# Half-block copies and z's stores move to ScalarE, and norm sums get y's bank 0.15 slots later: a prediction and its test

## The chip, the core and the metric

The kernel runs on one core of a Trainium2 chip. The core's engines each run one stream of instructions in order and meet at semaphores: TensorE (PE in the profile, with its weight loads as PEld), VectorE (DVE), ScalarE (ACT), GpSimd (POOL), and SyncE (SP), which here only issues DMAs. The metric is device time in microseconds for one execution, as the median of several.

## The reference

One layer of an encoder block on 2048 positions of width 1024. One wide projection of the normalized input gives the queries, keys and values of two attention mixers and their gates. Both mixers normalize each head of q and k, add a table of relative positions to the scores, and take a softmax over a window.

```python
h = rms_norm(x, norm_gain[layer])
proj = h @ w_in[layer]
qa, ka, va, qb, kb, vb, ga, gb, mg = jnp.split(proj, split_idx, axis=-1)
qa = head_rms_norm(qa.reshape(bsz, S, A_Q_HEADS, HEAD_DIM), q_norm_a[layer]) * scale
...
ya, _ = banded_attention(qa, ka, va, A_WINDOW, 1, rel_bias[:, :A_Q_HEADS], sink_a[layer])
ya = ya.reshape(bsz, S, A_WIDTH) * jax.nn.silu(ga)
...
for g, (window, dilation) in enumerate(B_GROUPS):      # (128, 1), (512, 4), (2048, 16)
    o, l = dilated_group(qb[:, :, g], kb[:, :, g], vb[:, :, g], window, dilation, ...)
alpha = jax.nn.softmax(jnp.stack(lses, axis=0), axis=0)
yb = jnp.sum(alpha[..., None].astype(x.dtype) * jnp.stack(outs, axis=0), axis=0)
yb = yb.reshape(bsz, S, B_WIDTH) * jax.nn.silu(gb)
...
merged = gates[:, :, 0] * br_a + gates[:, :, 1] * br_b
x = x + merged @ w_out[layer]
```

## The kernel before

**Numbers as pairs.** Operands of matmuls are split into a 16-bit high part and a 16-bit rest, so each product is three matmuls: high by high, high by rest, rest by high (XH, XL for the input; wh, wl for weights).

**Stages.** First the input is normalized, transposed and split. Then comes the long stage that the change touches: 14 units, each a group of heads, with 8 slots per unit. At the end the branches are projected, merged and sent through the output projection.

**Units.** A unit is "A" (mixer A, two units) or "B" with a group g of the three dilations. For each of four pairs of heads the order is g = 1, g = 2, g = 0. A unit's tokens are taken in blocks of 128: g = 1 has four sequences of four blocks, g = 2 sixteen sequences of one block, g = 0 one sequence of 16 blocks. In g = 1 and g = 0 a query's window begins half a block early, so key blocks are placed half a block off from the query blocks.

**A slot.** In each slot TensorE projects a pair of blocks into two banks of PSUM, pj: 2 x 24 matmuls on line 654. For each bank, ACT evacuates q and k (L672) and v's high part (L687), and DVE v's rest (L693), which empties the bank. For the pair, in this order: ACT squares (L700), DVE sums and guesses a reciprocal root (L705, L706, L262), POOL refines it in three rounds (newton, L271 to L274), DVE scales (L717), POOL multiplies by the gain (L724), ACT rounds to the high part (L730), DVE takes the rest (L734), POOL swaps the parts of k (L739), and SP transposes both blocks by DMA (L747) into a ring of eight blocks, kq, in two rows of four. Where one row ends and the next begins, the window of a query needs a half block again in the other row, or at the end of its own: `edge` copies it, 0.45 slots after the transpose. There are 36 such copies: per pair of heads 4 in g = 1 (L759) and 5 in g = 0 (L763, three of L757, L766). In slots of some units TensorE also does projections of gates as "fills" (L309).

**Attention of a block.** About three slots after its pair began: scores into PSUM (PE, L832), bias and maximum (DVE, L847), exponential (ACT, L855), high part and rest (ACT L860, DVE L864), transpose by DMA (SP, L870), values (PE, L881), and evacuation by ACT: L900 for mixer A, L905 for g = 0, and for g = 1 and 2 L909 into a tile z, which `z_store` sends to memory (L916, 0.1 slots later, 128 stores). In g = 0 the stored parts are read back (L890) and the three groups are merged: DVE makes factors (L1019 to L1032), POOL multiplies (three products per two blocks, L1037), DVE adds (L1043, L1044).

**The bank pt.** One bank of PSUM serves two uses in turn. `YPart.turn` transposes a finished part of y into it (PE, L943), and `YPart.gate` multiplies it by the gate (DVE, L947). Norm sums of weights, of gates and of y (`norm_sum`, L195, two tiny matmuls) use it too. The flag `held` keeps one from being placed between the other's write and read; a step that finds it set tries again 0.04 slots later.

**Order.** The order of each engine's instructions is written out by hand: steps are put on a heap with a due time in slots (`at`), and `until` takes them from it between two matmuls. The constants at the top are such times. The program then waits only through semaphores.

Of the kernel before, what the change touches and what calls it, by code (L numbers as in the profile page):

```python
# [24 lines left out]
AF = mybir.ActivationFunctionType  # L25
# [52 lines left out]
G_PREP = (5.907, 6.882, 7.102, 7.671, 7.712, 7.812, 7.942)  # L78
N_PREP = (6.3, 7.15, 7.753)
B_GAP = (0.25, 0.138, 0.231)  # L80
Y_MAX = (0.026, 0.815, 0.839)
X_SQ = (5.098, 1.401, 9.779, 2.051)
X_CH = (9.3, 2.65, 1.024, 0.955, 1.155, 1.305)
# [29 lines left out]
def block_kernel(tc, x, w_units, w_gate, w_mrg, w_brn, w_out, w_bra, gain, qkg, sink, bias_a, bias_b, b_merge, out):  # L113
    nc = tc.nc
    V = nc.vector
    A = nc.scalar
    G = nc.gpsimd
# [69 lines left out]
    held = [False, True]  # L187
# [128 lines left out]
    def g_load(c, raw=None, parts=(0, 1)):  # L316
        if raw is None:
            raw = sp0.tile([128, NCH, 128], F32, name="graw", bufs=2)[:]
        for i in parts:
            nc.sync.dma_start(out=raw[:, 4 * i:4 * i + 4, :], in_=w_gate[c][:, 4 * i:4 * i + 4, :])  # L320
        gw[c] = [raw]
# [44 lines left out]
    def gate_steps(ps, c, q, ih, m):  # L366
        th = []

        def tanh():
            th.append(gp.tile([128, 512], F32, name="yo", bufs=3))  # L370
            if m is None:
                A.activation(th[0][:], ps[:], AF.Tanh, scale=ih[:])
            else:
                i = 8 * (m % 2) + m // 2
                A.activation(th[0][:], ps[:], AF.Tanh, bias=bmh[:, i:i + 1], scale=ih[:])

        def gate():
            if m is None:
                V.scalar_tensor_tensor(th[0][:], th[0][:], 1.0, ps[:], OP.add, OP.mult)

        def store():
            d = gtd[c] if m is None else mgd[m]
            nc.sync.dma_start(out=d[:, 512 * q:512 * q + 512], in_=th[0][:])
            done.add(("gt", c, q))

        return tanh, gate, store
# [4 lines left out]
    def at(t, f, *args):  # L391
        seq[0] += 1
        heapq.heappush(heap, (t, seq[0], f, args))

    now = [0.0]
# [6 lines left out]
    def chain(steps):  # L402

        steps = sorted(steps, key=lambda e: e[0])
        done = [0]

        def go(k):
            if done[0] < k or steps[k][1](*steps[k][2:]) is False:
                at(now[0] + .04, go, k)
            else:  # L410
                done[0] = k + 1

        for k, e in enumerate(steps):
            at(e[0], go, k)
# [220 lines left out]
    ring = wk.tile([128, 6, 2 * RING], F16, name="kq", bufs=1)  # L635
    blocks = [0]

    class Pair:
# [113 lines left out]
        def edge(self, r, c, o):  # L752

            un = self.un
            if c:
                e = RING * (o < RING) + 512
                G.tensor_copy(ring[:, :un.nq, e:e + 64], ring[:, :un.nq, o:o + 64])  # L757
            elif un.n == 4:
                G.tensor_copy(ring[:, :, o + 512:o + 576], ring[:, :, o:o + 64])  # L759
                un.kq[r, 4] = ring, o + 512  # L760
            else:
                first = wk.tile([128, 6, 64], F16, name="kq0", bufs=1)
                G.tensor_copy(first[:], ring[:, :, o:o + 64])  # L763
                un.kq[r, un.n] = first, 0
            if c and c + 4 == un.n:
                G.tensor_copy(ring[:, :un.nq, o + 512:o + 576], un.kq[r, un.n][0][:, :un.nq, :])  # L766


    class Item:
# [142 lines left out]
        def z_store(self):  # L912
            un = self.un
            dst = zd[un.idx][un.g - 1].rearrange("(j d) f -> d j f", d=un.d)[
                self.r, 128 * self.i:128 * self.i + 128, :]
            nc.sync.dma_start(out=dst, in_=self.z[:].rearrange("p h f -> p (h f)"))  # L916
            done.add(("z", un.idx, un.g, self.r, self.i))


    class YPart:  # L920
# [10 lines left out]
        def plan(self, t):  # L931
            steps = [(t + d, f) for d, f in zip(Y_PART, (self.load, self.turn, self.gate, self.top, self.store))]
            if self.q == 3:
                steps += [(t + Y_PART[3] + d, f) for d, f in zip(Y_MAX, (self.max1, self.max2, self.max3))]
            chain(steps)

        def turn(self):
# [4 lines left out]
            for b in range(4):  # L942
                T.transpose(self.ps[:, 128 * b:128 * b + 128], self.y[:, b, :], idf[:])  # L943

        def gate(self):
            held[0] = False
            V.scalar_tensor_tensor(self.o[:], self.ps[:], gw[self.chunk][2][:], self.o[:],  # L947
                                   OP.mult, OP.mult)

# [139 lines left out]
    for u in range(NU + 1):  # L1089
        t = 8 * u  # L1090
        steps = [(t + W_STEP[0] + B_GAP[0] * i, w_load, u + 1, (i,)) for i in range(4)]
        for i in range(4):
# [6 lines left out]
    for c, u, slots in FILLS:  # L1099
# [6 lines left out]
        for i in range(2):  # L1106
            at(t + G_PREP[0] + B_GAP[1] * i, lambda u=u, c=c, i=i: g_load(c, pre[u][0], (i,)))
        chain([(t + G_PREP[1] + .1 * i, g_gain, c, i) for i in range(2)]
              + [(t + d, f, c) for d, f in zip(G_PREP[2:], (g_square, g_sum, g_pow, g_hi, g_lo))])
    for k in range(8):  # L1110
# [4 lines left out]
        for j in range(4):  # L1115
            at(t + N_PREP[0] + B_GAP[2] * j, piece_load, u, k, j)
        for half in range(2):
# [5 lines left out]
    un, nxt = None, 0.0  # L1123
    t = 0
    while t < NPAIR or heap or any(k >= t for k in fill):
        u, j = divmod(t, 8)
        steps = [(f, args) for f, *args in fill.pop(t, [])]
        if u < NU:
            if j == 0:
                un = Unit(u)  # L1130
# [5 lines left out]
            e = [t + 3.9 / (7.8 + 5.2 * len(steps)), t + 7.8 / (7.8 + 5.2 * len(steps))]  # L1136
# [272 lines left out]
    def gate_group(n):  # L1409
# [43 lines left out]
        def two(ps):  # L1453
            d = tile_()
            plus(d, ps, a, 1.0)
            gate(d, d, 0, 0, T_S[8])

        steps = ((A11, B11, lambda ps: copy(a, ps, 1.0)), (A12, B21, two), (S1, T1, lambda ps: copy(b, ps, 16.0)),
                 (S2, T2, lambda ps: (plus(c, ps, a, 16.0), add(a, b, c))),
                 (S3, T3, lambda ps: (plus(c, ps, c, 16.0), add(b, b, c), gate(b, b, 1, 2, T_S[7]))),  # L1460
                 (S4, B22, lambda ps: (plus(a, ps, a, 4.0), gate(a, a, 1, 0, T_S[8]))),
                 (A22, N4, lambda ps: (plus(c, ps, c, 4.0), gate(c, c, 0, 2, T_S[8]))))
# [106 lines left out]
    def branch_pair(i, dc, q):  # L1569
        set_, col = (i // 3, i % 3) if i < 6 else (2, i - 6)  # L1570
        assert ("br", set_) in done and all(("y", c, q) in done for c in range(8))
        for k in range(2):
            ps = ps_p.tile([128, 512], F32, name="fps")

            def product(ps=ps, k=k):
                g = gates[dc, q, k]
                V.scalar_tensor_tensor(g[:], g[:], 1.0, ps[:], OP.add, OP.mult)

            e = job(2.6, tproj_list(ps, *bw[set_][1:3], 128 * col, 0, 4, YS[q][0], YS[q][1], 4 * k))
            at(e + T_GATE[1], product)  # L1580

        def merge():
            m = gates[dc, q, 0]
            G.tensor_tensor(m[:], m[:], gates[dc, q, 1][:], OP.add)
            kept[dc, q] = m[:]

        at(e + T_GATE[2], merge)
        return e
# [12 lines left out]
    for k, (i, q) in enumerate(steps):  # L1601
        e = branch_pair(i, BCS[i], q)
        if k + 3 < len(steps):
            at(e + T_GATE[3], gate_load, BCS[steps[k + 3][0]], steps[k + 3][1])
        p = (i // 2, q % 2)
# [168 lines left out]
```

## Time and profile before

| | us |
| --- | --- |
| median of three runs | 1957.76 (1952.71 to 1959.26) |
| the profiled execution, its own time | 1958.9 |
| its span, first to last instruction | 1956.9 |
| PE busy | 1926.9 (98%) |
| DVE busy | 1377.4 (70%) |
| ACT busy | 1063.0 (54%) |
| POOL busy | 971.2 (50%) |

How to read it: times are microseconds from the start of the span. "L757" is line 757 of the kernel. A row of the timeline gives start, length, engine, line, operation, the tiles written and read, their shapes, and how many were merged; in square brackets stands how long the engine was idle before and what ended that. A row of waits gives who waited for whom, the total, the number of times and the longest. A row of a group has the busy time and the mean in ns behind the first bar. A row of one tile or line has minimum, median and maximum in ns. In rows of SP the length is that of the issue, not that of the transfer. The granted clock is TensorE's, as a share of its full speed.

### The profile page before, as it was taken

What the parts mean: (1) busy time and instruction counts of PE and PEld (TensorE: products, weight loads), DVE (VectorE), ACT (ScalarE), POOL (GpSimd) and SP (SyncE); (2) the same over time, 40 slices, a digit from 0 to 9 for tenths busy, and PEclk for the clock granted to TensorE, in tenths of its full rate; (3) what the DMA queues carried; (4) which work ended last, traced back from release to release, by engine and by line L of the source; (5) the groups of instructions that cost most, each with busy time, mean ns of one, the idle gap of its engine ahead of it and who ended that gap; (6) DMA issues with size and microseconds to landing.
All of it is one profiled execution on the core that took longest, in us unless ns stands there. A gap on an engine that the chain in (4) does not pass through costs nothing.

```text
span 1956.9 us, 40345 instructions
## 1 busy us (share of the span) xinstructions
PE 1926.9 (98%) x13702; PEld 1213.0 (62%) x13702; DVE 1377.4 (70%) x3604; ACT 1063.0 (54%) x2415; POOL 971.2 (50%) x2476
## 2 busy tenths in 40 slices
PE   8999999999999999999999899999999999999999
PEld 5556666677766688666787567876444444444444
DVE  6668777888768876677876878767776757877312
ACT  7457656776565566565666655656434545422100
POOL 4254556455556766647666676656511210232533
PEclk8999999999999999999999999999999999999999
DMA  6239977897848696677766776756722346788763
GB/s 251 81 77 174 188 151 160 137 189 144 180 98 187 117 189 127 124 148 163 156 132 145 143 167 123 144 121 119 175 83 85 107 163 195 223 245 264 259 221 143
DMA packets 589743, 307.97 MB, mean 157 GB/s; under 512 B 458080, under 2 KB 527328, under 8 KB 588256
## 3 DMA queue, kind: packets, MB, share of 16 engines
q1 hardware_dynamic: 589536, 305.39, 66.1%
q8 instruction: 107, 1.75, 0.4%
q14 instruction: 100, 0.82, 0.2%
HBM read 129.91 MB, written 65.27 MB: 100 GB/s over the span
## 4 chain that ended last, share of the span: by engine, by line
PE 82%; POOL 6%; DVE 5%; issue 3%; DMA 2%; ACT 1%; SPq 0%; POOLq 0%; DVEq 0%; ACTq 0%
PE pj L654 33%; PE pj L309 14%; PE fps L309 13%; PE fps L1641 7%; PE fps L1436 5%; PE s L832 4%; PE pv L881 4%; POOL rs_t L271 1%; POOL rs_t L272 1%; DVE qss L705 1%; POOL rs_t L273 1%; DVE rw L717 1%; POOL rw L724 1%; DMA kq<-spl 1%; POOL rs_y L274 1%
## 5 line engine op out<-in xcount | busy, mean ns | idle before, releaser
L654 PE MATMUL pj<-wh,XL 128*128 128x384 f16 x1792 | 587.2, 328 | 0.0
L654 PE MATMUL pj<-wh,XH 128*128 128x384 f16 x1792 | 585.3, 327 | 1.7 <-DVE vt L693 1.7
L654 PE MATMUL pj<-wl,XH 128*128 128x384 f16 x1792 | 585.9, 327 | 0.0
L654 PEld LDWEIGHTS <-XH 128*128 128x128 f16 x3584 | 413.2, 117 | 150.9 <-issue 3.9
L847 DVE CUSTOM_DVE_ANT_0 pr<-s,b,ubuf 128x256 f32<-128x256 f32 (+3 forms) x512 | 218.7, 464 | 60.7 <-PE s L832 59.3
L654 PEld LDWEIGHTS <-XL 128*128 128x128 f16 x1792 | 207.9, 116 | 69.2 <-issue 0.7
L864 DVE SCALAR_TENSOR_TENSOR p<-pr,p 128x512 f16<-128x512 f32 (+2 forms) x256 | 184.8, 722 | 20.7 <-ACT p L860 20.0
L271 POOL TENSOR_TENSOR rs_t<-rs_y 128x8 f32<-128x8 f32 (+2 forms) x345 | 103.8, 301 | 181.6 <-DVE rs_y L262 138.7
L717 DVE TENSOR_TENSOR rw<-rw,qr 128x512 f32<-128x512 f32 (+1 forms) x112 | 111.5, 996 | 90.1 <-POOL vt L680 50.7
L724 POOL TENSOR_TENSOR rw<-rw,g 128x128 f32<-128x128 f32 (+1 forms) x224 | 131.5, 606 | 71.4 <-DVE rw L717 60.0
L309 PEld LDWEIGHTS <-wh 128*128 128x128 f16 x960 | 94.2, 98 | 111.7 <-issue 2.6
L860 ACT ACTIVATE p<-pr 128x512 f16<-128x512 f32 (+2 forms) x256 | 159.6, 623 | 7.1 <-issue 0.3
L832 PE MATMUL s<-kq 128*128 128x256 f16 (+3 forms) x1168 | 148.3, 255 | 11.1 <-POOL kq L757 11.1
L739 POOL COPY spl<-spl 128x256 f16<-128x256 f16 (+1 forms) x224 | 94.2, 450 | 120.7 <-DVE spl L734 120.1
L309 PE MATMUL fps<-Y,wh 128*128 128x512 f16 x512 | 152.2, 379 | 0.0
L881 PEld LDWEIGHTS <-pt 128*128 128x128 f16 x3024 | 125.7, 97 | 35.0 <-issue 0.2
L309 PE MATMUL pj<-XH,gh 128*128 128x512 f16 x384 | 146.0, 380 | 0.0
L309 PE MATMUL pj<-XL,gh 128*128 128x512 f16 x384 | 145.8, 380 | 0.0
L309 PE MATMUL pj<-XH,gl 128*128 128x512 f16 x384 | 145.8, 380 | 0.0
L672 ACT ACTIVATE rw<-pj 128x256 f32<-128x256 f32 (+1 forms) x224 | 86.3, 385 | 109.2 <-PE pj L654 107.4
L1641 PE MATMUL fps<-wt,M 128*128 128x512 f16 (+1 forms) x684 | 145.2, 375 | 0.0
L730 ACT ACTIVATE spl<-rw 128x512 f16<-128x512 f32 (+1 forms) x112 | 72.2, 644 | 131.9 <-POOL vt L680 86.1
(245 smaller groups left out, 3691.3 us busy)
## 6 DMA issues: line engine op xcount, KB each, us to landing
wraw<-in_w_units_dram SPq DMA_DIRECT2D x56, 384.0 KB, 4.6
mtd<-mm SPq DMA_DIRECT2D x56, 256.0 KB, 3.7
M<-mtd SPq DMA_DIRECT2D x8, 1792.0 KB, 9.4
mgd<-fg SPq DMA_DIRECT2D x39, 256.0 KB, 2.1
zd<-z SPq DMA_DIRECT2D x128, 66.0 KB, 1.9
zz<-zd SPq DMA_DIRECT2D x64, 132.0 KB, 2.7
xt<-in_x_dram SPq DMA_DIRECT2D x16, 512.0 KB, 8.7
gtd<-yo SPq DMA_DIRECT2D x32, 256.0 KB, 2.9
```

The source lines that it names most:

```text
L271: G.tensor_tensor(tv, yv, yv, OP.mult)
L309: out.append(lambda w=w, xx=xx, ch=ch, i=i: T.matmul(ps[:], lhsT=w[:, ch, c0:c0 + 128], rhs=xx[:, ch, ts], start=(i == 0), stop=(i == n - 1)))
L654: out.append(lambda lhs=lhs, rhs=rhs, ch=ch, k=k: T.matmul(ps[:, :384], lhsT=lhs[:, ch, :], rhs=rhs[:, ch, :], start=(k == 0), stop=(k == ...
L717: V.tensor_tensor(q, q, self.rr[:, :n].unsqueeze(2).to_broadcast([128, n, HD]), OP.mult)
L724: G.tensor_tensor(q[:, i, :un.nq, :], q[:, i, :un.nq, :], g, OP.mult)
L832: T.matmul(self.sv[j][:, o:o + k1 - k0], lhsT=q[:, h, qo:qo + 128], rhs=kt[:, un.nq + kh + v * un.nk, k0:k1], start=(v == 0), stop=(v == 1))
L847: V.tensor_tensor_reduce(out=self.pv[:, j, self.p0:self.p0 + W], in0=self.sv[j], in1=un.bias[:, self.h0 + j, self.b0:self.b0 + W], scale=I ...
L860: A.activation(self.sp[:, :128 * n], self.pr, AF.Copy, scale=PSC)
L864: V.scalar_tensor_tensor(self.sp[:, 128 * n:], self.pr, PSC, self.sp[:, :128 * n], OP.mult, OP.subtract)
L881: T.matmul(self.po[:, j, :w], lhsT=p[:, n * j + s, :], rhs=un.v[key][:, vh, c0:c0 + w], start=(k == 0 and s == 0), stop=(k == 2 and s == n ...
L1436: mm.append(lambda ch=ch, k=k, w=w, i=i: T.matmul(ps[:], lhsT=weight(bl, ch)[w], rhs=xblock(x, ch)[k], start=(i == 0), stop=(i == 11)))
L1641: mm.append(lambda ch=ch, k=k, w=w, i=i: T.matmul(ps[:, :cols.stop - cols.start], lhsT=m[:, a, ch, k, :], rhs=wt[w][:, b, ch, cols], start ...
```

## The change

Three things change. The copies of half blocks in `edge` are issued on ACT, as activations with the function Copy, at the same due time. `z_store` issues its DMA from ACT's queue, not SP's, at the same due time. And `gate` clears `held` not at once but 0.15 slots later, so that a norm sum (or another part's transposes) is placed that much later in TensorE's order.

```diff
+Y_FREE = 0.15
...
             if c:
                 e = RING * (o < RING) + 512
-                G.tensor_copy(ring[:, :un.nq, e:e + 64], ring[:, :un.nq, o:o + 64])
+                A.activation(ring[:, :un.nq, e:e + 64], ring[:, :un.nq, o:o + 64], AF.Copy)
             elif un.n == 4:
-                G.tensor_copy(ring[:, :, o + 512:o + 576], ring[:, :, o:o + 64])
+                A.activation(ring[:, :, o + 512:o + 576], ring[:, :, o:o + 64], AF.Copy)
                 un.kq[r, 4] = ring, o + 512
             else:
                 first = wk.tile([128, 6, 64], F16, name="kq0", bufs=1)
-                G.tensor_copy(first[:], ring[:, :, o:o + 64])
+                A.activation(first[:], ring[:, :, o:o + 64], AF.Copy)
                 un.kq[r, un.n] = first, 0
             if c and c + 4 == un.n:
-                G.tensor_copy(ring[:, :un.nq, o + 512:o + 576], un.kq[r, un.n][0][:, :un.nq, :])
+                A.activation(ring[:, :un.nq, o + 512:o + 576], un.kq[r, un.n][0][:, :un.nq, :], AF.Copy)
...
-            nc.sync.dma_start(out=dst, in_=self.z[:].rearrange("p h f -> p (h f)"))
+            nc.scalar.dma_start(out=dst, in_=self.z[:].rearrange("p h f -> p (h f)"))
...
+        def free(self):
+            held[0] = False
+
         def gate(self):
-            held[0] = False
+            at(now[0] + Y_FREE, self.free)
             V.scalar_tensor_tensor(self.o[:], self.ps[:], gw[self.chunk][2][:], self.o[:],
                                    OP.mult, OP.mult)
```

## The prediction

> **What bounds the kernel now.** I read the page's busy shares first, then TensorE's own waits, then the granted clock around those waits, and last the timelines of the other engines there.
>
> ```profile
> span 1956.9 us, 40345 instructions
> PE 1926.9 (98%) x13702; PEld 1213.0 (62%) x13702; DVE 1377.4 (70%) x3604; ACT 1063.0 (54%) x2415; POOL 971.2 (50%) x2476
> ...
> PE s L832 <- POOL kq L757: 11.1, 5, 3.8
> ...
> PE pt L195 <- DVE yo L947: 3.4, 2, 1.8
> PE pj L654 <- DVE vt L693: 1.7, 3, 0.9
> ```
>
> TensorE (PE) is busy for 98% of the span and idle for 30.0 us (1956.9 - 1926.9). Nothing that the change does to ScalarE (ACT), GpSimd (POOL) or SyncE's queue (SP) counts unless it shortens or adds one of PE's waits. Two of the waits shown are touched: 11.1 us in five waits for the copied half block (L757), and 3.4 us in two waits in which a norm sum (L195) needs the bank that y's gate (L947) still reads. Together that is 14.5 us, 0.74% of the span.
>
> A wait can cost more than its own length, as the windows behind three of them show (columns: stretch, length, busy time and count of PE, PEld, DVE, ACT, POOL, then the granted clock and DMA).
>
> ```profile
> 512.40:515.81 3.41, 3.41 (x14) 2.03 (x13) 2.47 (x15) 1.67 (x5) 1.12 (x4) 0.50 1.25 203
> 1113.26:1116.60 3.34, 3.34 (x16) 2.04 (x17) 3.27 (x9) 1.30 (x4) 3.11 (x6) 0.51 1.11 251
> 1386.20:1389.60 3.40, 3.40 (x9) 1.22 (x8) 2.19 (x8) 2.75 (x6) 0.98 (x3) 0.50 1.15 314
> 1360.77:1364.20 3.43, 3.43 (x37) 2.40 (x38) 3.36 (x9) 2.32 (x7) 3.11 (x6) 1.00 0.42 81
> ...
> 291.31 0.38 PE L195 MATMUL pt<-ym,ones 128*128 128x1 f32 x2 [1.58 <-DVE yo L947]
> 511.15 0.38 PE L195 MATMUL pt<-ym,ones 128*128 128x1 f32 x2 [1.84 <-DVE yo L947]
> 1113.26 1.03 PE L832 MATMUL s<-kq 128*128 128x128 f16 x8 [3.79 <-POOL kq L757]
> 1360.77 0.34 PE L832 MATMUL s<-kq 128*128 128x128 f16 x3 [2.81 <-POOL kq L757]
> 1384.93 0.62 PE L832 MATMUL s<-kq 128*128 128x128 f16 x8 [2.31 <-POOL kq L757]
> ```
>
> After the waits of 1.84, 3.79 and 2.31 us the clock is granted at half for some 3.4 us. Work that takes 3.4 us at half speed would take 1.7 us, so each of the three loses another 1.7 us: 5.1 us that stand under "busy". The 2.81 us wait is followed by full clock, so length alone does not decide it. The most that the change can free is thus 14.5 + 5.1 = 19.6 us.
>
> **The copies.** There are 36 of them. Their prices on POOL, and those of ACT's nearest work of the same sizes:
>
> ```profile
> L759 POOL COPY kq<-kq x16: 504/505/1029, 224.1 to 1229.3; 128x384 f16<-128x384 f16 x16
> L757 POOL COPY kq<-kq x12: 285/291/748, 568.8 to 1384.1; 128x128 f16<-128x128 f16 x12
> ...
> L855 ACT ACTIVATE pr<-pr,nmA 128x384 f32<-128x384 f32 x112 | 62.5, 609 | 1.8 <-DVE nmA L847 1.7
> L855 ACT ACTIVATE pr<-pr,z 128x128 f32<-128x128 f32 x128 | 44.2, 398 | 8.0 <-DVE z L847 8.0
> ```
>
> ACT's copy is not cheaper: I take 0.40 us for the small ones and 0.61 us for the large, from its exponentials of those sizes (bounds 0.29, as on POOL, and 0.61). What changes is the queue that the copy stands in. Here is the worst wait, on POOL and on ACT:
>
> ```profile
> 1110.12 2.65 POOL L1037 TENSOR_TENSOR zz<-zz,bm_e 128x256 f32<-128x256 f32 x3
> 1112.76 0.45 POOL L757 COPY kq<-kq 128x128 f16<-128x128 f16 x1
> 1113.30 1.04 POOL L724 TENSOR_TENSOR rw<-rw,g 128x128 f32<-128x128 f32 x2
> ...
> 1108.56 0.91 ACT L855 ACTIVATE pr<-pr,nmB 128x256 f32<-128x256 f32 x2 [1.70 <-DVE nmB L847]
> 1114.37 0.63 ACT L730 ACTIVATE spl<-rw 128x512 f16<-128x512 f32 x1 [4.07 <-DVE bm_n L1020]
> 1380.41 0.91 ACT L855 ACTIVATE pr<-pr,nmB 128x256 f32<-128x256 f32 x2 [1.44 <-DVE nmB L847]
> ```
>
> On POOL the copy stands behind 2.65 us of products (L1037). On ACT the same place in program order is behind L855, which ends at 1109.47, and ACT then idles 4.07 us before L730. The copy would end near 1109.9, about when PE begins to wait (1113.26 - 3.79 = 1109.47). So 3.3 us of that wait go at this point.
>
> Not all of it is kept. In this stretch the chain newton, scale, gain (L724), hi (L730), lo, swap runs on POOL, DVE and ACT at its own pace, and only the copy's 0.45 us leaves it. PE, arriving earlier, next meets the bank of pj:
>
> ```profile
> 1129.23 0.28 DVE L693 SCALAR_TENSOR_TENSOR vt<-pj,vt 128x128 f16<-128x128 f32 x1
> 1130.35 0.33 PE L654 MATMUL pj<-wh,XH 128*128 128x384 f16 x1
> ```
>
> That matmul opens a group in the bank that L693 empties, and has 1130.35 - 1129.51 = 0.84 us to spare. If L693 comes only 0.4 us earlier, PE keeps 0.84 + 0.4 = 1.2 us of the two waits before 1117 (1.58, not shown, and 3.79) and of the half clock. Bounds: nothing, where the later wait brings a half-clock window itself, and all of 1.6 + 3.8 + 1.7 = 7.1 us. I take 1.2, because the rows behind L693 are back to back.
>
> The last three waits (0.6, 2.81 and 2.31 us, plus one half-clock window of 1.7) come to 7.4 us. At 1384.93 the copy on ACT would follow L855, which ends at 1380.41 + 0.91 = 1381.3; with 0.40 for the copy and 0.3 for a transpose that may land last, PE goes on at 1382.0 instead of 1384.9. That is 2.9 us for the three together, as PE comes early and waits for the rest anyway; with the half clock gone, 4.6 us. Bounds 2.0 and 7.4. **Copies: 1.2 + 4.6 = 5.8 us gained** (2.0 to 14.5).
>
> The copies' own waits move too, and that is their cost. They wait for the transposes that SP issues:
>
> ```profile
> L747 SPq DMA_TRANSPOSE kq<-spl x224: 1209/1232/2633, 101.9 to 1389.9; - x112
> ...
> POOL kq L759 <- DMA kq<-spl: 23.4, 9, 5.4
> ```
>
> Nine large copies wait 23.4 us on POOL, 2.6 us each. On ACT what is queued behind them is the exponentials' rounding (L860), z's evacuation (L909), and pj's evacuation (L672, L687), on which DVE's L693 and then PE wait. The cover is ACT's idle time, 46% of the span by the page. Where it lacks, a copy late by 2.6 us delays PE by that minus what pj has to spare. I take nothing here, counting on that idle time (bounds 0 and, with two delays of 1 us per unit in the four units that have four large copies each, 8 us).
>
> **The stores of z.** 128 issues leave SP for ACT. SP's rows, the load of ACT in a stretch with two stores per slot, and two of pj's margins there (the first and the last of the seven openings of a bank between 740 and 800 us with under 1.5 us to spare):
>
> ```profile
> L916 SPq DMA_DIRECT2D zd<-z x128: 320/524/1972, 272.6 to 1338.9; - x128
> ...
> 740.00:800.00 60.00, 60.00 (x477) 47.73 (x476) 40.66 (x137) 38.71 (x109) 35.94 (x127) 1.00 0.73 149
> ...
> 740.12 0.28 DVE L693 SCALAR_TENSOR_TENSOR vt<-pj,vt 128x128 f16<-128x128 f32 x1
> 741.44 0.33 PE L654 MATMUL pj<-wh,XH 128*128 128x384 f16 x1
> ...
> 793.70 0.28 DVE L693 SCALAR_TENSOR_TENSOR vt<-pj,vt 128x128 f16<-128x128 f32 x1
> 794.29 0.33 PE L654 MATMUL pj<-wh,XH 128*128 128x384 f16 x1
> ```
>
> ```profile
> SPq L429 <- DMA xt<-in_x_dram: 5.7, 6, 1.0
> ```
>
> No ACT-issued DMA is in this trace. I price one by SP's median, 0.52 us; bounds 0.32 and 1.97. Ahead of it stand its own L909 and, as the loads of x (L429) show, which fill fresh tiles and still wait for older loads, an older transfer that uses the same completion semaphore: 1.0 us at the longest there. Behind a store on ACT stand L672 and L687, so a late store is a late L693. The margins are 1.0 and 0.3 us, and the store costs most of them only if ACT has no idle time in front of L672; ACT is busy for 38.7 of 60 us. I take 1 us lost in all (bounds 0 and about 20, see the rivals). SP gets 128 x 0.52 = 67 us of its queue back; no wait of PE names a transfer, so I count nothing for that.
>
> **The norm sums.** The sum now follows y's gate directly, and PE waits 1.58 and 1.84 us for DVE. Put 0.15 slots later, PE does other work first. A slot has 48 projection matmuls, which start 0.16 us apart:
>
> ```profile
> 1108.98 0.33 PE L654 MATMUL pj<-wh,XL 128*128 128x384 f16 x1
> 1109.14 0.33 PE L654 MATMUL pj<-wh,XH 128*128 128x384 f16 x1
> ```
>
> That makes 7.7 us, some 9 us with scores and values, so 0.15 slots are 1.35 us. What is left of the waits is 0.2 and 0.5 us, and the half-clock window behind the second goes: **1.35 + 1.35 + 1.7 = 4.4 us gained** (1.0, if the window stays and the next sum is late in its turn, to 5.1). A later sum makes weights' scales later (L202 on), which are due over a slot afterwards.
>
> **Sum.** -5.8 - 4.4 + 1.0 = -9.2 us: the span goes from 1956.9 to 1947.7. The profiled run took 1958.9 us, 1.1 above the median of the runs, 1957.76, so the median becomes **1948.6 us**, 0.47% faster.
>
> The Trainium skill, "TensorE: Matmul & The Clock Gate", Part 1, says that the clock falls to half after an idle window of about 3.4 us. The rows disagree: 1.84 us was enough at 511, and 2.81 us was not at 1360. By the rule, the wait that I expect to remain near 1126 to 1130 costs only itself; by the rows it could add 1.7 us, which makes 1950.3.
>
> **The rivals.**
>
> *The waits only move* (0.25). What speaks for it: the stretches around 1113 and 1360 are paced by POOL, DVE and ACT, of which the copy is 0.4 us per slot. Then PE keeps 0.4 us at each of the five copies, 2 us, the norm sums bring 1.35 us, the clock still drops once after each: 1957.8 - 3.4 = 1954.4 us. Against it: ACT has 4.07 us idle just where the copy goes.
>
> *All of it goes* (0.13): 19.6 us less, and 1 us for the stores, 1939.2 us. For it: nothing but L693 and L747 stands behind those waits. Against it: the 0.84 us margin.
>
> *The stores hold ACT* (0.15), the one on the slower side. SP's transposes take 1.2 us each to issue, and a store follows them closely:
>
> ```profile
> 758.59 2.54 SPq L747 DMA_TRANSPOSE kq<-spl  x2
> 761.22 0.53 SPq L916 DMA_DIRECT2D zd<-z  x1
> ```
>
> If one issue must wait for the other, a store holds ACT for 0.52 + 1.2 = 1.7 us. Two of them in a slot of 9 us on an engine that is busy 65% leave it nearly full, L672 is late by 1 to 2 us in each slot, and PE's margins of 0.3 to 1.0 us are overrun by some 0.6 us. One such opening per slot (seven in the 60 us above), 32 slots in the four units like that one: 32 x 0.6 = 20 us. 1948.6 + 20 = 1968.6 us. It decides from about 1.2 us per store; below, the margins hold. Against it: the smallest issue took 0.32 us, and ACT idles for 46% of the span.
>
> [...]
>
> **How the numbers follow.** Less than 0.3%, 5.9 us, cannot be told from no change here: the runs of before spread over 6.6 us. The forecast (0.47) holds 1944 to 1952 with its bounds for the kept parts. Faster is the forecast and the case in which all goes, less a little for the forecast's upper edge: 0.58. Within 0.3% are the moved waits and that edge: 0.27. Slower is the stores' case: 0.15. The range must leave out no more than 0.2: 1941 to 1964 leaves out most of the slower case and half of the case in which all goes.
>
> **What would show it.** Right: PE's wait for kq falls from 11.1 us to under 4 and names ACT; L195's waits fall under 1 us; two or three windows of half clock after 500 us are gone; a wait on L693 appears near 1130. Stores on ACT show 0.3 to 0.6 us. Wrong: stores above 1.2 us with PE's waits on L693 growing past 10 us (slower), or kq's waits unchanged in sum with POOL's L724 as early as before (moved).

## The result, and the profile after

| | before | after |
| --- | --- | --- |
| median, us | 1957.21 (1952.71 to 1959.71, 7 runs) | 1949.72 (1947.51 to 1949.9, 7 runs) |
| ratio after/before | | 0.996 (95% interval 0.9948 to 0.9971) |
| profiled execution: own time, span | 1958.9, 1956.9 | 1949.46, 1947.7 |

The change made the kernel 0.40% faster. The predicted time was 1948.6 us, the predicted span 1947.7. That they agree so closely is partly luck: the experiments show that one of the three terms behind the forecast is empty and another is made of different waits.

The page of the changed kernel, its head and PE's waits (engine, line waited for: total, times, longest):

```profile
span 1947.7 us, 40273 instructions
PE 1923.5 (99%) x13702; PEld 1211.9 (62%) x13702; DVE 1373.0 (70%) x3604; ACT 1073.4 (55%) x2451; POOL 953.4 (49%) x2440
...
PE pj L655 <- DVE vt L694: 6.2, 6, 2.0
PE s L833 <- ACT kq L758: 2.0, 3, 1.2
...
PE pt L196 <- DVE yo L951: 0.9, 1, 0.9
```

Lines have moved by one, below the gate by four: L757 is now L758, L654 is L655, L693 is L694, L195 is L196, L947 is L951, L916 is L917. PE is idle for 24.2 us (1947.7 - 1923.5) instead of 30.0. The wait for kq fell from 11.1 to 2.0 us, the norm sums' from 3.4 to 0.9, and the wait for pj's bank (vt) grew from 1.7 to 6.2 us. PE's own rows in the timeline of the changed kernel show where:

```profile
289.55 0.38 PE L196 MATMUL pt<-ym,ones 128*128 128x1 f32 x2
508.38 0.38 PE L196 MATMUL pt<-ym,ones 128*128 128x1 f32 x2 [0.85 <-DVE yo L951]
1085.39 0.62 PE L833 MATMUL s<-kq 128*128 128x128 f16 x8 [1.20 <-ACT kq L758]
1104.83 0.62 PE L833 MATMUL s<-kq 128*128 128x128 f16 x8 [0.46 <-ACT kq L758]
1112.95 0.32 PE L655 MATMUL pj<-wh,XH 128*128 128x384 f16 x1 [1.99 <-DVE vt L694]
1125.33 0.32 PE L655 MATMUL pj<-wh,XH 128*128 128x384 f16 x1 [1.05 <-DVE vt L694]
1360.06 0.32 PE L655 MATMUL pj<-wh,XH 128*128 128x384 f16 x1 [1.91 <-DVE vt L694]
1377.40 0.62 PE L833 MATMUL s<-kq 128*128 128x128 f16 x8 [0.34 <-ACT kq L758]
```

The first row has no bracket: that sum waits for nothing to speak of, where it waited 1.58 us before. In the stretch from 1080 to 1130 us, waits for kq of 5.4 us became 1.7 us for kq and 3.0 for the bank. In the stretch from 1330 to 1390 us, 5.7 us became 2.9 (with 0.7 for a part of y, not shown). Of the three half-clock windows after 200 us one is left, behind the wait at 1112.95. The two parts that moved, in the view of one line (min/median/max in ns):

```profile
L917 ACTq DMA_DIRECT2D zd<-z x128: 326/326/379, 268.9 to 1333.7; - x128
...
L758 ACT ACTIVATE kq<-kq x12: 292/294/308, 565.3 to 1377.0; 128x128 f16<-128x128 f16 x12
...
L760 ACT ACTIVATE kq<-kq x16: 506/507/524, 223.8 to 1224.1; 128x384 f16<-128x384 f16 x16
...
  DMA kq<-spl: 5.7, 3
```

A store takes ACT 0.33 us, none of the 128 more than 0.38. The last row is what ended ACT's idle time before the large copies: three waits for transposes, 5.7 us. On POOL it was nine waits and 23.4 us.

### The profile page after: what moved, and what is told of

Read it like the earlier page. It is cut to its first block, busy times and chain, and to the rows that moved or that the text cites. A ratio compares the mean times of both kernels' runs of the same rounds, so it can differ in the third digit from the quotient of the medians.

```text
span 1947.7 us, 40273 instructions
## 1 busy us (share of the span) xinstructions
PE 1923.5 (99%) x13702; PEld 1211.9 (62%) x13702; DVE 1373.0 (70%) x3604; ACT 1073.4 (55%) x2451; POOL 953.4 (49%) x2440
## 4 chain that ended last, share of the span: by engine, by line
PE 49%; DVE 4%; POOL 3%; issue 2%; ACT 1%; DMA 1%; SPq 0%; DVEq 0%; POOLq 0%
PE pj L655 16%; PE fps L310 13%; PE fps L1645 7%; PE pj L310 6%; PE fps L1440 5%; PE s L833 1%; PE pv L882 1%; POOL rs_t L272 1%; POOL rs_t L273 1%; DVE rw L718 1%; DVE qss L706 1%; POOL rs_t L274 1%; DMA kq<-spl 0%; POOL rs_y L275 0%; DVE pr L848 0%
## 5 line engine op out<-in xcount | busy, mean ns | idle before, releaser
L655 PE MATMUL pj<-wh,XH 128*128 128x384 f16 x1792 | 584.7, 326 | 6.2 <-DVE vt L694 6.2
L655 PE MATMUL pj<-wh,XL 128*128 128x384 f16 x1792 | 586.6, 327 | 0.0
L655 PE MATMUL pj<-wl,XH 128*128 128x384 f16 x1792 | 585.2, 327 | 0.0
L655 PEld LDWEIGHTS <-XH 128*128 128x128 f16 x3584 | 412.9, 117 | 155.1 <-issue 8.1
L655 PEld LDWEIGHTS <-XL 128*128 128x128 f16 x1792 | 207.8, 116 | 68.8 <-issue 0.2
L865 DVE SCALAR_TENSOR_TENSOR p<-pr,p 128x512 f16<-128x512 f32 (+2 forms) x256 | 185.9, 726 | 25.1 <-ACT p L861 24.2
```

The source lines that it names most:

```text
L655: out.append(lambda lhs=lhs, rhs=rhs, ch=ch, k=k: T.matmul(ps[:, :384], lhsT=lhs[:, ch, :], rhs=rhs[:, ch, :], start=(k == 0), stop=(k == ...
L865: V.scalar_tensor_tensor(self.sp[:, 128 * n:], self.pr, PSC, self.sp[:, :128 * n], OP.mult, OP.subtract)
```

## The experiments

All ratios are to the kernel before, run on the same chip in the same session; they can differ by up to 0.0006 from the quotient of the two medians. Over three sessions its median was 1954.2, 1953.6 and 1954.1 us (81 runs), 3 us below the first seven.

**The parts alone.** First, the copies alone:

```diff
-                G.tensor_copy(ring[:, :un.nq, e:e + 64], ring[:, :un.nq, o:o + 64])
+                A.activation(ring[:, :un.nq, e:e + 64], ring[:, :un.nq, o:o + 64], AF.Copy)
```

(and so for the other three copies)

> Only the copies move to ScalarE; the stores stay on SyncE's queue and the norm sums where they were. My account: the copies are worth what they gained between 1080 and 1390 us in the changed kernel, about 5 us (0.7 in the earlier pair of slots, 4.4 in the later one), so 1952 us, ratio 0.9974; PE's wait for kq falls from 11.1 to about 2 us, and 5 to 6 us of waits for pj's bank (DVE's vt) appear; the two norm sums still wait 1.6 and 1.8 us. Rival (the waits only move): 2 us gained, 1955 us, with kq and vt together waiting as long as before, about 11 us. Rival (ScalarE is held by the copies' own waits for the transposes): slower than 1957.

Measured: 1950.05 us, 0.9977 (0.9968 to 0.9986), 4.5 us faster, as expected. The waits for kq and for the bank are as expected too (the bank's 1.7 us grew by 5.9):

```profile
PE pj L654 <- DVE vt L693: 7.6, 7, 2.4
...
PE s L832 <- ACT kq L757: 2.1, 3, 0.8
PE pt L195 <- DVE yo L947: 1.6, 1, 1.6
```

The last row is a surprise: without any later norm sum, one of the two sums no longer waits.

The stores alone:

```diff
-            nc.sync.dma_start(out=dst, in_=self.z[:].rearrange("p h f -> p (h f)"))
+            nc.scalar.dma_start(out=dst, in_=self.z[:].rearrange("p h f -> p (h f)"))
```

> Only the stores of z move to ScalarE's queue. My account: 0.33 us each on ScalarE and no lock, so within 1 us of the kernel before, 1956 to 1958 us, with PE's five waits for kq and the two norm sums as before. Rival of the prediction (stores hold ScalarE): 1.2 us each or more and waits for vt of over 10 us, 1977 us. Third possibility (SyncE's free 67 us bring transposes and loads sooner): 1 to 3 us faster.

Measured: 1953.27 us, 1.0 (0.9991 to 1.0009). The interval leaves room for neither a loss nor a gain of more than 1.8 us. An issue took ScalarE 0.33 us, 0.38 at most.

The norm sums alone:

```diff
+Y_FREE = 0.15
...
-            held[0] = False
+            at(now[0] + Y_FREE, self.free)
```

> Only the bank of y goes to the norm sums 0.15 slots later. My account: the two waits of 1.6 and 1.8 us fall to under 0.2 and about 0.9, and the half-clock window behind the second goes: 2.5 + 1.7 = 4.2 us gained, 1953 us, ratio 0.9979; kq waits as before. Rival (the later sums delay the scales of the next weights): a new wait for wh, wl or gh on PE of over 1 us, and no gain beyond 2 us.

Measured: 1953.67 us, 0.9999 (0.999 to 1.0008). A miss: neither the expected 4.2 us nor the rival's new wait. The two sums wait as before, 3.0 us together:

```profile
PE pt L196 <- DVE yo L951: 3.0, 2, 1.5
```

**Two parts together.** Copies and norm sums, the stores as before:

> The change without its stores: copies on ScalarE and later norm sums, z's stores still from SyncE. My account, with the parts adding up: within 1 us of the whole change, 1949 to 1951 us. If the prediction's term for the stores (1 us lost) is right, it is 1 us faster than the whole change, 1948.7; if the stores gained by freeing SyncE, 1 to 3 us slower, 1951 to 1953.

Measured: 1949.3 us, 0.9977 (0.9967 to 0.9986), the same as the copies alone. Copies and stores, the norm sums as before, beside the whole change again:

> The change without the later norm sums. My account now: Y_FREE = 0.15 left the two waiting sums at their old places in PE's order (the order of matmuls around them is the same with and without it) and moved one sum of wsq alone, so this runs as the whole change does, within 1 us, with waits of about 0.1 and 0.9 us at those two sums. The prediction's account (the sums moved by 1.35 us): 4.4 us slower than the whole change, waits of 1.4 and 2.2 us.

> The whole change once more, beside the runs of before that the parts are measured against. If the parts add up (copies 4.5 us, norm sums and stores nothing, as the first four runs have it): 1949.8 us where before is 1954.2, ratio 0.9977. If copies and stores help each other (the load of y leaves SyncE some 1.2 us earlier once z's stores are out of its queue, which shortens the second norm sum's wait): 1 to 3 us more, ratio 0.9962 to 0.9972.

Measured: copies and stores 1949.1 us, 0.9971 (0.9959 to 0.9983); the whole 1947.89 us, 0.9966 (0.9954 to 0.9979). The later norm sums are worth nothing that can be seen; the prediction's account wanted 4.4 us. Whether the stores add 1 to 2 us once the copies are off POOL stays open, since 0.9977, 0.9971 and 0.9966 overlap.

Why the norm sums did not move is in the order of PE's instructions: with and without Y_FREE = 0.15 it differs in one place, a sum of wsq near 1420 us, which comes 19 matmuls later. The two sums of ym keep their places. A step that finds `held` set tries again 0.04 slots later; these two were due more than 0.15 slots after the gate anyway. At 0.2 slots the program places them two matmuls later, at 0.4 twelve.

**Norm sums that do move.** The kernel before with

```diff
+Y_FREE = 0.4
```

> The kernel before with the norm sums alone, but 0.4 slots later, which puts 12 matmuls (1.9 us) ahead of both waiting sums. If the prediction's price per wait was right and only the distance too short: both waits gone, 2.5 to 3.4 us gained, and the half-clock window behind the second in those executions that have it, so 1950 to 1952 where before is 1954.2, ratio 0.9977 to 0.9988. If the waits are not on the way to the end (taken up by a later wait): ratio 0.9995 or more.

Measured: 1958.28 us, 1.0021 (1.0012 to 1.003), 4 us slower. Both accounts missed. PE's rows (the first two) and DVE's around the first sum:

```profile
289.49 0.28 PE L196 MATMUL pt<-ym,ones 128*128 128x1 f32 x2
293.31 0.56 PE L196 MATMUL pt<-gsq,ones 128*128 128x1 f32 x2 [3.19 <-DVE wm L203]
...
288.43 0.74 DVE L951 SCALAR_TENSOR_TENSOR yo<-pt,ubuf,yo 128x512 f32<-128x512 f32 x1
293.01 0.15 DVE L203 TENSOR_REDUCE wm<-pt 128x1 f32<-128x1 f32 x1
```

The sum of ym waits no more, but the next user of the same bank, the sum of gsq, keeps its place, and now waits 3.19 us until DVE has read the first. The wait was handed to the next in line, longer than it was. The same happens after the second sum, where the next sum of gsq waits 2.02 us (at 516.08 us). Together that is 5.2 us in place of 3.4, and in this profile half clock follows both waits, for two stretches of 3.4 us behind the first and one behind the second.

**Which copies, and why.** Only the 20 large copies on ACT:

```diff
             elif un.n == 4:
-                G.tensor_copy(ring[:, :, o + 512:o + 576], ring[:, :, o:o + 64])
+                A.activation(ring[:, :, o + 512:o + 576], ring[:, :, o:o + 64], AF.Copy)
...
-                G.tensor_copy(first[:], ring[:, :, o:o + 64])
+                A.activation(first[:], ring[:, :, o:o + 64], AF.Copy)
```

> The kernel before with only the 20 large copies (lines 759 and 763) on ScalarE; the small ones stay on GpSimd at their old place. My account: the large copies, waiting up to 5.4 us for their transposes at the head of GpSimd's queue, held newton and through scale and y's gate the first norm sum. So the wait near 290 us goes (under 0.3 us instead of about 1.5), the one near 510 stays within 0.5 us of 1.5, the five waits for kq stay at 10 to 11 us together; 1 to 2 us gained, ratio 0.999 to 0.9995, and the half-clock window behind it never comes. Rival (the first norm sum's wait varies by chance from run to run): 1 us or more is left at 290.

Measured: 1950.55 us, 0.9983 (0.9974 to 0.9992), 3.3 us faster, more than expected. The first norm sum, as the timeline has it, in the kernel before:

```profile
281.60 0.50 POOL L759 COPY kq<-kq 128x384 f16<-128x384 f16 x1 [5.41 <-DMA kq<-spl]
285.19 0.20 POOL L274 TENSOR_TENSOR qr<-rs_t,rs_y 128x8 f32<-128x8 f32 x1
...
285.43 0.69 DVE L717 TENSOR_TENSOR rw<-rw,qr 128x512 f32<-128x512 f32 x1 [1.70 <-POOL qr L274]
290.52 0.74 DVE L947 SCALAR_TENSOR_TENSOR yo<-pt,ubuf,yo 128x512 f32<-128x512 f32 x1
```

and with the large copies on ACT:

```profile
280.70 0.20 POOL L274 TENSOR_TENSOR qr<-rs_t,rs_y 128x8 f32<-128x8 f32 x1
...
281.96 0.68 DVE L717 TENSOR_TENSOR rw<-rw,qr 128x512 f32<-128x512 f32 x1
287.05 0.74 DVE L947 SCALAR_TENSOR_TENSOR yo<-pt,ubuf,yo 128x512 f32<-128x512 f32 x1
287.89 0.34 PE L195 MATMUL pt<-ym,ones 128*128 128x1 f32 x2
```

Before, POOL stood 5.41 us at the head of its queue, waiting for the transposes that L759 copies. Newton (up to L274) is behind it, DVE waits 1.70 us for Newton before L717, y's gate (L947) is behind L717, and the norm sum waits 1.58 us for the gate. With the copy gone from POOL, L717 starts without a wait and the norm sum without one too. PE's waits for kq stay, as the small copies are where they were:

```profile
PE s L832 <- POOL kq L757: 10.4, 4, 3.8
```

The 1.5 us at the first norm sum are less than half of the 3.3 us. The rest is not traced to a wait. This profile has one half-clock window after 200 us where that of the kernel before has three, but such windows differ between executions of one kernel (see the last section).

The small copies stay on POOL but are due earlier:

```diff
-                    at(now[0] + KQ_COPY, self.edge, r, c, o)
+                    at(now[0] + KQ_COPY - 0.20 * (c > 0), self.edge, r, c, o)
```

> The small copies (of blocks after the first) stay on GpSimd but are due 0.2 slots earlier, ahead of the 2.2 to 2.65 us of products (L1037) instead of behind them. If the place in the queue set the cost, not the engine: the waits of 3.8, 2.8 and 0.8 to 2.3 us at the last slots of the two stretches fall by 2.2 to 2.6 us each until pj's bank stops PE, 3 to 4 us gained, ratio 0.998 to 0.9985, less than with ScalarE because the large copies still hold GpSimd while they wait for the transposes (the first norm sum keeps its wait of about 1.5 us). If GpSimd waits for the transposes at the earlier place: newton is late, vt's waits grow, ratio 0.9995 or more.

Measured: 1953.15 us, 0.9992 (0.9983 to 1.0001); less than expected. POOL's rows at the worst place, and the waits:

```profile
1109.25 0.29 POOL L757 COPY kq<-kq 128x128 f16<-128x128 f16 x1
1109.50 2.64 POOL L1037 TENSOR_TENSOR zz<-zz,bm_e 128x256 f32<-128x256 f32 x3
...
PE pj L654 <- DVE vt L693: 7.3, 6, 2.4
PE pt L195 <- DVE yo L947: 4.2, 2, 2.5
PE s L832 <- POOL kq L757: 3.3, 4, 1.5
```

The place in the queue did set the wait for kq: ahead of the 2.64 us of products, 11.1 us became 3.3, with the copy on the same engine. But the bank's wait took 7.3 us, as with ACT, and the norm sums got worse (4.2 us).

**The stores' price.** The whole change, and behind each store five tiny copies on ACT whose result nobody reads:

```diff
+            [A.activation(hold[:], hold[:], AF.Copy) for _ in range(5)]
```

> The whole change, and behind each store of z five tiny copies of 128x16 on ScalarE (about 0.2 us each, nothing reads their result), so that a store holds ScalarE for 0.33 + 1.0 = 1.3 us. The prediction's rival put the point from which held stores decide at 1.2 us and their price at 20 us. If that sizing is right: waits for vt in the units with stores, 10 to 25 us slower than the whole change, 1958 to 1973 us. If ScalarE's idle time covers them: within 2 us of the whole change, 1948 to 1950.

Measured: 1954.58 us, 1.0003 (0.9993 to 1.0013), against 0.9966 for the whole change (on another chip): 3.7 per mille, some 7 us slower (3 to 12 by the two intervals). Between the two expectations. PE's waits, and the tiny copies:

```profile
PE pj L655 <- DVE vt L694: 10.1, 9, 2.4
...
PE pt L196 <- DVE yo L951: 3.0, 2, 1.9
...
L917 ACT ACTIVATE hold<-hold x640: 198/215/220, 268.0 to 1343.3; 128x16 f16<-128x16 f16 x160
```

Five of them take 1.2 us in a row, more than the expected 1.0, so that a store held ACT for some 1.5 us.

**The bank first.** In the last unit of each pair, DVE empties pj's bank (L694) before it forms the low halves (L735); in the second kernel the low part of the gate's weights (L356) goes behind both as well:

```diff
-                    at(e[i] + d, f, i)
+                    at(e[i] + d - 0.04 * (f == self.v_lo and self.un.kind == "B" and self.un.g == 0), f, i)
...
-                at(e[1] + d, f)
+                at(e[1] + d + (0.103 * (f == self.lo) + 0.037 * (f == self.swap)) * (self.un.kind == "B" and self.un.g == 0), f)
```

```diff
-G_PREP = (5.907, 6.882, 7.102, 7.671, 7.712, 7.812, 7.942)
+G_PREP = (5.907, 6.882, 7.102, 7.671, 7.712, 7.812, 8.09)
```

> The whole change, and in the last units of each pair (B, g = 0) VectorE empties pj's bank (L694) before it forms the low halves (L735) instead of after. My account: the copies' gain is capped by the wait for this bank, three or four waits of 2.0, 1.1 to 2.4 and 1.6 to 1.9 us; each falls by 0.6 to 0.7 us, and the half-clock window near 1113 to 1125, which needs about 1.9 us idle in one stretch of 3.4 us, is rarer: 2 to 3.5 us gained on the whole change, 1945 to 1946 us, ratio to before 0.9948 to 0.9956. Rival (the chain newton, scale, hi, lo, turn sets the pace and L735 is on it): later low halves give the time back as waits for kq, within 1 us of the whole change.

> As the run before, and the low part of the gate's weights (L356, 1.28 us on VectorE) is due 0.15 slots later, behind the bank and the low halves. My account: the waits near 1125 and 1370 fall by another 1.3 us each and no half-clock window comes in either stretch; 1 to 3 us less than the run before, 1943 to 1945 us, ratio to before 0.9938 to 0.995. Rival (the gate's matmuls then wait for gl, or the chain sets the pace): no better than the run before.

Measured: 1949.28 us, 0.9976 (0.9966 to 0.9985), and 1949.34 us, 0.9972 (0.9962 to 0.9982). Neither is better than the whole change; the expected 2 to 3.5 us did not come. The first one's waits:

```profile
PE pj L655 <- DVE vt L694: 5.8, 5, 1.8
PE s L833 <- ACT kq L758: 3.6, 4, 1.3
```

The bank's waits fell (from 6.2 and 7.2 us in the two profiles of the whole change to 5.8, and to 4.1 in the second kernel) and no half-clock window is left after 200 us in either profile, but the wait for kq grew from 2.0 and 2.1 to 3.6 us, and to 3.9 in the second. The rival holds as far as the waits go: what is taken from the bank comes back at kq.

## Why the prediction came out right, and where its steps did not

The table adds up PE's waits from its rows in the timeline of each profile, by place, and counts the half-clock windows of 3.41 us between 200 and 1940 us (1.7 us each).

| kernel | sum near 290 | sum near 510 | 1080 to 1135 us | 1325 to 1395 us | half-clock windows |
| --- | --- | --- | --- | --- | --- |
| before | 1.6 | 1.8 | 5.4 | 5.7 | 3 |
| norm sums alone | 1.5 | 1.5 | 5.3 | 3.9 | 3 |
| stores alone | 1.0 | 1.1 | 5.2 | 4.1 | 2 |
| large copies alone | 0 | 1.4 | 5.3 | 5.1 | 1 |
| copies alone | 0 | 1.6 | 6.0 | 3.2 | 1 |
| copies, norm sums | 0.1 | 1.2 | 5.9 | 2.6 | 1 |
| copies, stores | 0.3 | 1.4 | 5.8 | 2.7 | 1 |
| whole, first profile | 0.1 | 0.9 | 4.7 | 2.9 | 1 |
| whole, second profile | 0 | 1.1 | 6.0 | 2.8 | 1 |

**What bounds the kernel.** Right: PE's few waits and the half clock behind them carry the difference. Of the 9.2 us between the two spans, 5.8 are idle time of PE (30.0 - 24.2) and 3.4 its busy time (1926.9 - 1923.5), as much as two half-clock windows cost.

**The norm sums, 4.4 us.** This is the step that failed: "Put 0.15 slots later, PE does other work first." The sums kept their places, and alone the part is worth 0.2 us (from 2.0 gained to 1.6 lost). The first sum's wait went all the same, by the copies: the large ones no longer hold POOL, hence Newton, L717 and the gate. The second sum's wait varies, 1.5 to 1.8 us with copies and stores as before and 0.9 to 1.6 with one or both moved. Part of it is the load of y that the gate needs, which SP issues earlier once the stores are gone, as the rows of SP and of the gate before and after show:

```profile
505.73 0.56 SPq L929 DMA_DIRECT2D yo<-gtd  x1
510.34 0.75 DVE L947 SCALAR_TENSOR_TENSOR yo<-pt,ubuf,yo 128x512 f32<-128x512 f32 x1 [1.18 <-DMA yo<-gtd]
...
501.92 0.57 SPq L930 DMA_DIRECT2D yo<-gtd  x1
507.58 0.75 DVE L951 SCALAR_TENSOR_TENSOR yo<-pt,ubuf,yo 128x512 f32<-128x512 f32 x1
```

PE reached the sum at 509.31 us before (511.15 - 1.84) and at 507.53 after (508.38 - 0.85), so the load is issued 5.6 us ahead of PE instead of 3.6; with the stores alone moved it is 5.4, with the copies alone 3.4. In all seven profiles with the stores on SP, DVE idles 0.9 to 2.2 us before this gate until the load has landed; in the seven with the stores on ACT it does not. So "no wait of PE names a transfer, so I count nothing for that" was too quick: DVE's gate waited for that load, and PE for the gate. That this is worth time is not shown; alone, the stores gain nothing that can be measured.

**The copies, 5.8 us.** The size was nearly right (4.5, interval 2.7 to 6.3), its make-up was not. The term was made of PE's waits for the small copies (L757) alone and gave the large ones no gain. By the times it is rather the other way round: the large ones alone gain 3.3 us (1.6 to 5.1), which leaves 1.2 us for the small ones, though the two intervals overlap.

Place by place: from 1080 to 1135 us the term was 1.2 gained; in four of five profiles with all copies moved PE waits 0.4 to 0.8 us longer there, in one 0.5 to 0.7 less. There the rival of moved waits won: the predicted wait on L693 appeared, at 1112.95 and 1125.33 us, and it takes everything. From 1325 to 1395 us the term was 4.6; the profiles with the small copies on POOL lose 5.1 to 7.4 us there with the half clock counted, those with all copies on ACT 2.6 to 3.2, so 2 to 4.8 us are right.

The first norm sum adds 1.5 us that the term did not have. The prediction showed the row for it, 23.4 us of POOL waiting for transposes, and asked only what that wait would do to ACT. What it did to the engine that it left was not asked. On ACT it shrank to 5.7 us, and no loss shows there, as taken: PE's waits between 700 and 1080 us went from 1.4 to 0.9 us.

**The stores, 1 us lost.** None was. An issue took 0.33 us, near the lower bound of 0.32, not the 0.52 of SP's median, and 0.38 at most, so no waiting for SP's transposes, which took 1.2 us each, shows in it. The rival's price for held stores was too high: with 1.5 us per store, near its 1.7, some 7 us are lost and not 20. In the profile PE's waits for the bank between 700 and 1080 us grew from 0.9 to 3.5 us (not the predicted 0.6 us in each of 32 slots), the norm sums lost 2.0 us, and there is one half-clock window more. Where held stores begin to decide, which the prediction put at 1.2 us, is not shown more closely than between 0.33 and 1.5 us.

**Why the total agreed.** By luck, in part. The prediction took the change from one execution with three half-clock windows, 1958.9 us, where the median of 81 later runs is near 1954. Run again beside such runs, the whole change gains 6.6 us by the ratio (4.1 to 9.0), not 9.2. The 9.2 us held two of the three windows as gained, 3.4 us: one in the norm sums' term, behind the wait at 511.15, one in the copies', behind that at 1384.93. Executions with such waits need not have them: with the norm sums alone the second sum still waits 1.5 us and no half clock follows; with the large copies alone the last small copy is still waited for, 2.28 us, and none follows either.

## What to carry to other kernels

When an instruction that waits for a transfer leaves an in-order queue, ask first who stood behind it there: here PE waited for no large copy, and moving them took away the first norm sum's wait of 1.5 us. The row that shows where to look is the idle time before the instruction on the old engine. When a due time is moved in a program that retries, compare the orders of the two programs before counting a gain; 0.15 slots moved neither of the sums that waited. And a stretch that is paced by a chain over several engines can hand a wait on from one resource to the next, as from kq to the bank near 1113 us and back to kq with the bank first, so the length of the wait that is removed is not yet the gain.

## What the runs showed of the clock

The half clock goes by a fixed grid of stretches of 3.413 us, not by the length of one wait. In the kernel before, the three windows start at 512.40, 1113.14 and 1386.21 us, which is 176.0 and 80.0 stretches apart. These are the stretches of that grid around three waits (columns: stretch, length, busy time of PE, PEld, DVE, ACT, POOL, granted clock, DMA share, GB/s):

```profile
508.98:512.39 3.41, 1.57 (x14) 1.29 (x13) 2.16 (x7) 2.04 (x5) 2.42 (x12) 1.00 1.02 292
512.39:515.81 3.42, 3.42 (x14) 2.04 (x13) 2.48 (x15) 1.67 (x5) 1.12 (x4) 0.50 1.24 202
1355.49:1358.90 3.41, 2.46 (x25) 1.43 (x23) 2.35 (x8) 1.71 (x4) 2.83 (x10) 1.00 0.83 179
1358.90:1362.31 3.41, 1.54 (x15) 1.15 (x16) 3.24 (x6) 0.43 (x1) 3.41 (x8) 1.00 0.58 110
1362.31:1365.72 3.41, 3.41 (x34) 2.23 (x32) 3.34 (x12) 3.41 (x9) 2.31 (x5) 1.00 0.04 7
1382.79:1386.21 3.42, 1.28 (x12) 0.85 (x13) 3.28 (x7) 0.00 (x0) 3.42 (x7) 1.00 1.10 223
1386.21:1389.62 3.41, 3.41 (x9) 1.22 (x8) 2.20 (x8) 2.75 (x6) 0.97 (x3) 0.50 1.15 312
```

The wait of 2.81 us at 1360.77 is cut in two by the grid, 0.95 and 1.87 us, and costs nothing more; that of 1.84 us at 511.15 lies in one stretch and costs the next one. Over the profiles of this study, between 200 and 1940 us, a stretch at full clock with less than 1.8 us of idle PE was never followed by half clock, one with more than 2.05 us always; between them both occurred (1.87 and 2.03 without, 1.81 and 1.84 with). From half clock, 1.1 us of idle time was enough to stay there (in the kernel with norm sums 0.4 slots later, two windows in a row from 292.2 us), 0.5 us was not. The Trainium skill, "TensorE: Matmul & The Clock Gate", Part 1, calls the window free-running, and these rows agree; the prediction had held its 3.4 us against single waits. The prediction was right that a wait of 1.84 us can be enough: no stretch had to be idle throughout.

The grid's phase differs between executions: the window near 1113 us begins at 1113.14 in the profile of before and at 1113.58 in that of after. So the same wait can cost 1.7 us more in one run and nothing more in the next. The wait for kq at 1360.77 is 2.8 us long in five profiles; half clock follows it with the stores alone and with the norm sums alone, and does not in the kernel before, with the large copies alone and with norm sums 0.4 slots later.

The granted clock goes with part of the spread from run to run. Of the 81 later runs of the kernel before, the five with a mean granted clock of 0.994 have a median of 1956.1 us, the ten with 0.998 one of 1952.7, 3.4 us less. It does not explain all of the spread: the 30 runs with 0.997 still go from 1951.0 to 1955.9 us.
